# Attention with a state space mixer: state space products placed between the value products

## The chip, the cores and the metric

One Trainium2 chip, one core. The metric is the device time of one execution in microseconds (us). Before the change the median of three executions is 3305.14 us (3303.23 to 3305.94). The engines are called as in the profile: PE is TensorE (matmuls; PEld its weight loads), DVE is VectorE, ACT is ScalarE, POOL is GpSimd, SP is SyncE, which here only issues DMAs.

## The reference, cut to what matters

One layer of a diffusion backbone serves 2048 latent and 256 context tokens of width 1024. A combined projection gives grouped-query attention (8 query heads, 2 key heads of 64) and the input of a complex-diagonal state space (32 channel groups of 16, each with a 64-dimensional complex state, forward and backward). The change touches the stretch in which both are computed at the same time:

```python
s = einsum("bqkgd,bskd->bkgqs", q_blk, k) * scale
p = softmax(s)                                   # over latent and context keys
attn = einsum("bkgqs,bskd->bqkgd", p, v)

xr = einsum("blgh,gph->blgp", u, bbr)            # state inputs (real, imaginary)
_, _, hr, hi = associative_scan(_combine, (ar, ai, xr, xi), reverse=reverse)
y  = einsum("blgp,ghp->blgh", hr, c_re) - einsum("blgp,ghp->blgh", hi, c_im)
...
out = g * sigmoid(g @ w_glu + b_glu)             # g = gelu(y + d * u)
```

After it come the GLU, the output projection, and a SwiGLU feed-forward layer of width 2816.

## The kernel before, in words

**Attention.** There are 20 units: 4 for the context queries (2 key tiles each) and 16 for the latent queries (512 queries, two heads, 20 key tiles of 128 each). `attend` cuts each unit's key tiles into groups of 4, so a latent unit has 5 groups. For each key tile, a *slot* (`slot`) runs the score products of two heads (L266 and L267) into one of two PSUM buffers `st`, and ACT turns them into `p` by an exponential (L269). Then the slot takes steps of a second generator B, which prepares a later unit: above all products of queries and keys whose maximum is wanted (L197, PE) and the reduction of each by DVE (`mx`, L198). These go through a ring `m` of three PSUM banks (`pmx`, bufs=3), which the state space products and a few others share. The slots of group g+1 stand ahead of the *values* of group g (`values`, L283: products of `p` with the values, 16 matmul records a group; L293 and L296 sum up `p` on DVE and POOL). After them come the steps of `finish` (row sums L317, a small chain of DMAs through DRAM for reciprocals, the scaling of the result L335).

**State space.** A third generator, `Sg` (`side`, whose first part is `ssm_gen`), is stepped once in every latent slot, with `X["pos"] = "p"`, and once at a group's end, with `X["pos"] = "v"`: 25 steps a latent unit. It works through 16 units of two channel groups. One unit needs:

- *state inputs* (L1012): for each direction d, 8 matmul records into a bank `m`, copied by ACT into `s` (L1016, L1017); then two DMAs `sw<-s` (L1021, L1022) that swap the halves;
- on DVE a rotation (L1032 to L1034, which writes `s` in place), the scan (L1040), two DMAs `rw<-r` (L1042, L1043), a rotation back (L1047, which writes `r` in place, L1048, L1052), and copies into `h` on ACT (L1059);
- *state outputs* (L982, L984): for each group g, 16 records into a bank `m`, copied by ACT into `ys` (L985), then 16 DMAs `y_scr<-ys` (L990) in all;
- `load` of the next unit: `mst`, `ut`, `et` (2 DMAs), `mot` and `wt` (8 DMAs), each tile with two buffers.

Before the change these are placed by counting steps. A unit takes 20 steps, which is 4 groups: its two input chunks and the two output chunks of the unit before it fall into the four slots of one group, directly behind score products and L197 products; L1032 to L1034, the scan, L1047 with L1048, and L1052 stand at the ends ("v") of four successive groups.

**Order.** The orders of PE and DVE are the program's (`manual_schedule`). ACT, POOL and SP also run strictly in an order fixed when the kernel is built, but there a planner sets it: it goes by its own cost of each instruction and issues, of those that it holds ready, the one that stands earliest in the program. So a load may be issued well ahead of its place, as soon as its buffer is free.

The functions that the change touches are these:

Of the kernel before, what the change touches and what calls it, by code (L numbers as in the profile page):

```python
# [8 lines left out]
F32 = mybir.dt.float32  # L9
F32R = mybir.dt.float32r  # L10
AF = mybir.ActivationFunctionType
# [8 lines left out]
CL, CC = NLAT // T, NCTX // T  # L20
NCH = CL + CC
NE = CL + 1 + CC + 1
# [3 lines left out]
NU = 16  # L26
# [22 lines left out]
def build(nc, tc, I, O):  # L49
    V, S, G, PE = nc.vector, nc.scalar, nc.gpsimd, nc.tensor  # L50
# [61 lines left out]
            f()  # L112

    pb, pe_, pst_, pps = ExitStack(), ExitStack(), ExitStack(), ExitStack()
    X = {"pos": "p"}
    KK = {}

    def attention_open():
        kc = pe_.enter_context(tc.tile_pool(name="kc", bufs=1, side="right"))
        pmx = pps.enter_context(tc.tile_pool(name="pmx", bufs=3, space=PSUM, side="right"))  # L120
        X.update(kc=kc, pmx=pmx)
        X["zb"] = [kc.tile([128, 4, 128], F32, name=f"zb{i}") for i in range(2)]
        for z in X["zb"]:
            G.memset(z, 0.0)

    def run(g):
        for _ in g:
            pass

    def kbuild(kv, t0, t1, part=None):  # L130
        n_ = t1 - t0
        if (kv, t0) not in KK:
            pool = X["kp"] if kv and n_ > 2 else X["kc"]
            khl = pool.tile([128, n_ * 128], F32R, name=f"khl{kv}_{t0}")
# [139 lines left out]
    def values(ui, j):  # L274
        kv, tok, nq, k0, k1, pr_ = units[ui]
        nk = k1 - k0
        if j == 0:
            PV[ui] = X["ppv"].tile([128, 512], F32, name="pv")
            ACC[ui] = {}
        pv, acc = PV[ui], ACC[ui]  # L280
        p = pts.pop((ui, j))
        for h in range(2):
            PE.matmul(pv[64 * h:64 * h + 64, 0:nq], X["vall"][:, k0 + j, 64 * kv:64 * kv + 64], p[:, h, 0:nq],  # L283
                      start=j == 0, stop=j == nk - 1)
        if nk <= 4:
            e = "v"
        elif ui + 1 == len(units):
            e = "v" if j % 3 == 2 or j > 16 else "g"
        else:
            e = "v" if j in VJ else "g"  # L290
        if e in acc:
            if e == "v":
                V.tensor_add(acc[e][:, :, 0:nq], acc[e][:, :, 0:nq], p[:, :, 0:nq])  # L293
            else:
                for h in range(2):
                    G.tensor_add(acc[e][:, h, 0:nq], acc[e][:, h, 0:nq], p[:, h, 0:nq])  # L296
        else:
            acc[e] = p
        if j == nk - 1:
            pvs = X["wk"].tile([128, 512], F32, name="pvs", bufs=2)  # L300
            S.copy(pvs[:, 0:nq], pv[:, 0:nq])
            PEND.append((ui, pvs, acc))
# [43 lines left out]
    def attend(B, Sg):  # L346
        groups = []
        for ui, u_ in enumerate(units):
            js = [(ui, j) for j in range(u_[4] - u_[3])]
            groups += [js[i:i + GROUP] for i in range(0, len(js), GROUP)]  # L350
        st = dict(ready=0, q=0.0, per=0.0, goal=1, s=0.0)
        fin = []

        def step():
            st["ready"] = next(B) or st["ready"]

        def slot(ui, j):
            while st["ready"] < ui:
                step()
            lat = units[ui][2] > 256  # L360
            if lat and not j:
                st["goal"] = min(ui + (2 if ui + 1 < 2 * len(cu) else 1), len(units) - 1)
                st["per"] = sum(prep_steps(i) for i in range(st["ready"] + 1, st["goal"] + 1)) / 19.5
                st["q"] = 0.0
            scores(ui, j)
            st["q"] += st["per"] if lat else 0.0
            while st["q"] >= 1.0:
                st["q"] -= 1.0
                if st["ready"] < st["goal"]:
                    step()  # L370
            if lat:
                X["pos"] = "p"
                next(Sg, None)

        for s_ in groups[0]:
            slot(*s_)
        for gi, g in enumerate(groups):
            if gi + 1 < len(groups):
                for s_ in groups[gi + 1]:
                    slot(*s_)  # L380
            for s_ in g:
                values(*s_)
            for f in list(fin):
                if next(f, "end") == "end":
                    fin.remove(f)
            if gi + 1 < len(groups) and len(groups[gi + 1]) > 2:
                X["pos"] = "v"
                next(Sg, None)
            if PEND:
                fin.append(finish())  # L390
        run(Sg)
        return fin
# [544 lines left out]
    sm = ps_.enter_context(tc.tile_pool(name="sm", bufs=1, side="right"))  # L937
# [5 lines left out]
    def ssm_gen():  # L943
# [7 lines left out]
        h0 = sm.tile([128, 2, 32], F32, name="h0")  # L951
        nc.scalar.dma_start(out=h0, in_=I["h0"])
        stt = sm.tile([128, 2, 32], F32, name="stt")
        dg4 = "p (d g) a -> p d g a"
        fl = "p a b -> p (a b)"
        got = {}
# [32 lines left out]
                for l in range(8):  # L989
                    nc.sync.dma_start(out=y_scr[32 * u + 16 * g:32 * u + 16 * g + 16, l::8, :], in_=ys[16 * l:16 * l + 16, g])  # L990

        def wait(n):
            for _ in range(n):
                yield

        load(0)
        yield from wait(10)
        while X["pos"] != "v":
            yield
        yield  # L1000
        for u in range(NU):
            gu = slice(2 * u, 2 * u + 2)
            mst, mot, wt, et, ut = got[u]
            s = sm.tile([128, 4, NE], F32, name="s", bufs=1)
            s4 = s.rearrange(dg4, d=2)
            S.copy(s4[:, :, :, 0], h0[:, :, gu])
            S.activation(s4[:, :, :, CL + 1], h0[:, :, gu], AF.Copy, scale=0.0)
            for d in range(2):
                sp_ = X["pmx"].tile([128, 2, NCH], F32, name="m")
                for g in range(2):  # L1010
                    for J in range(2):
                        PE.matmul(sp_[:, g, :], mst[:, 2 * d + g, 128 * J:128 * J + 128], ut[:, g, J, :], start=J == 0, stop=J == 1)  # L1012
                a, b = sp_[:, :, 0:CL], sp_[:, :, CL:NCH]
                if d:
                    a, b = a[:, :, ::-1], b[:, :, ::-1]
                S.copy(s[:, 2 * d:2 * d + 2, 1:CL + 1], a)  # L1016
                S.copy(s[:, 2 * d:2 * d + 2, CL + 2:NE], b)  # L1017
                if not d:
                    yield
            sw = sm.tile([128, 4, NE], F32, name="sw", bufs=1)  # L1020
            nc.sync.dma_start(out=sw[0:64], in_=s[64:128])  # L1021
            nc.sync.dma_start(out=sw[64:128], in_=s[0:64])  # L1022
            am = sm.tile([128, 4, NE], F32, name="am", bufs=1)
            G.tensor_mul(am.rearrange(dg4, d=2), lm[:, :, gu, None].to_broadcast([128, 2, 2, NE]), amask[:, None, None, :].to_broadcast([128, 2, 2, NE]))
            yield
            if u:
                yield from outputs(u - 1)
                yield
            else:
                yield from wait(2)  # L1030
            sw4 = sw.rearrange(dg4, d=2)
            V.tensor_mul(s4, s4, et[:, :, 0])  # L1032
            V.scalar_tensor_tensor(sw4, sw4, sg[:, 0:1], et[:, :, 1], op0=ALU.mult, op1=ALU.mult)
            V.tensor_add(s, s, sw)  # L1034
            yield
            if u + 1 < NU:
                load(u + 1)
            yield from wait(4)
            r = sm.tile([128, 4, NE], F32, name="r", bufs=1)
            V.tensor_tensor_scan(r.rearrange(fl), am.rearrange(fl), s.rearrange(fl), 0.0, op0=ALU.mult, op1=ALU.add)  # L1040
            rw = sm.tile([128, 4, NE], F32, name="rw", bufs=1)
            nc.sync.dma_start(out=rw[0:64], in_=r[64:128])  # L1042
            nc.sync.dma_start(out=rw[64:128], in_=r[0:64])  # L1043
            yield
            yield from wait(4)
            r4, rw4 = r.rearrange(dg4, d=2), rw.rearrange(dg4, d=2)
            V.tensor_mul(r4, r4, et[:, :, 0])  # L1047
            V.scalar_tensor_tensor(rw4, rw4, sg[:, 0:1], et[:, :, 1], op0=ALU.mult, op1=ALU.mult)  # L1048
            yield
            yield from wait(4)  # L1050
            h = sm.tile([128, 4, NCH], F32, name="h", bufs=1)
            V.tensor_sub(r.rearrange(fl), r.rearrange(fl), rw.rearrange(fl))  # L1052
            for d in range(2):
                dg = slice(2 * d, 2 * d + 2)
                for lo, hi, e0 in ((0, CL, 0), (CL, NCH, CL + 1)):
                    o = h[:, dg, lo:hi]
                    if d:
                        o = o[:, :, ::-1]
                    S.copy(o, r[:, dg, e0:e0 + hi - lo])  # L1059
            S.copy(stt[:, :, gu], r4[:, :, :, NE - 1])  # L1060
            yield
        yield from outputs(NU - 1)
        yield
        nc.sync.dma_start(out=O["st"], in_=stt.rearrange("p a b -> p (a b)"))
# [83 lines left out]
    Sg = side()  # L1148
# [475 lines left out]
    for i, (c, j) in enumerate(seq):  # L1624
        a, v = aq, vs
# [108 lines left out]
```

## Time and profile before

| what | value |
|---|---|
| median of three executions | 3305.14 us |
| the profiled execution | 3301.18 us |
| its span, first to last instruction | 3299.4 us |
| PE busy | 3063.7 us, 93% of the span |
| DVE, POOL, ACT busy | 77%, 57%, 41% |
| attention with the state space | about 456 to 1466 us of the span |

The span is 1.8 us shorter than the execution. A busy row says only that an engine had something in it; what ends an engine's idle time is read from the waits, and where the work stands from the rows in order of time (the timeline). In a timeline a row may merge several like instructions; its time is that from the first one's start to the last one's end, and matmuls overlap, so the pace is read from the starts of successive rows.

### The profile page before, as it was taken

What the parts mean: (1) busy time and instruction counts of PE and PEld (TensorE: products, weight loads), DVE (VectorE), ACT (ScalarE), POOL (GpSimd) and SP (SyncE); (2) the same over time, 40 slices, a digit from 0 to 9 for tenths busy, and PEclk for the clock granted to TensorE, in tenths of its full rate; (3) what the DMA queues carried; (4) which work ended last, traced back from release to release, by engine and by line L of the source; (5) the groups of instructions that cost most, each with busy time, mean ns of one, the idle gap of its engine ahead of it and who ended that gap; (6) DMA issues with size and microseconds to landing.
All of it is one profiled execution on the core that took longest, in us unless ns stands there. A gap on an engine that the chain in (4) does not pass through costs nothing. (4 is left out here: it accounts for less than half of the span.)

```text
span 3299.4 us, 46241 instructions
## 1 busy us (share of the span) xinstructions
PE 3063.7 (93%) x16087; PEld 2471.0 (75%) x16087; DVE 2552.3 (77%) x3444; ACT 1340.5 (41%) x2378; POOL 1885.7 (57%) x1373
## 2 busy tenths in 40 slices
PE   7898889999999999997997999999999999999797
PEld 5787765555655565557777999899989997878586
DVE  4899766777777887668778877987787877577887
ACT  4333334444444444544555333433343434232332
POOL 3767526655775686774435544554455555354675
PEclk9899999999999999998998999999999999999899
DMA  7565452323333322215565444444434446657653
GB/s 265 181 204 189 144 132 55 88 74 87 85 81 90 82 74 53 65 48 164 186 184 186 130 118 118 134 133 118 120 106 128 122 127 191 155 157 192 174 198 137
DMA packets 515379, 435.19 MB, mean 132 GB/s; under 512 B 106374, under 2 KB 449454, under 8 KB 515148
## 3 DMA queue, kind: packets, MB, share of 16 engines
q1 hardware_dynamic: 498060, 400.57, 40.4%
q0 software_dynamic: 5184, 18.88, 3.4%
q10 hardware_dynamic: 11904, 12.82, 1.2%
q8 instruction: 127, 2.08, 0.3%
q14 instruction: 104, 0.85, 0.1%
HBM read 279.37 MB, written 143.73 MB: 128 GB/s over the span
## 5 line engine op out<-in xcount | busy, mean ns | idle before, releaser
L296 POOL TENSOR_TENSOR p<-p 128x512 f32<-128x512 f32 x442 | 646.2, 1501 | 288.7 <-PE pv L283 185.1
L89 POOL TENSOR_TENSOR op<-wr,op 128x512 fp32r<-128x512 f32 (+1 forms) x297 | 413.9, 1401 | 402.8 <-ACT op L88 375.3
L94 PE MATMUL o<-h,op 128*128 128x384 f32 x1848 | 621.3, 336 | 17.8 <-ACT h L88 17.1
L95 PE MATMUL o<-h,op 128*128 128x384 f32 x1848 | 621.4, 336 | 16.7 <-DVE h L89 16.7
L96 PE MATMUL o<-h,op 128*128 128x384 f32 x1848 | 620.1, 336 | 0.0
L198 DVE TENSOR_REDUCE mx<-m 128x1 f32<-128x512 f32 (+1 forms) x656 | 404.8, 675 | 132.1 <-PE m L197 130.9
L269 ACT ACTIVATE p<-st 128x1024 f32<-128x1024 f32 (+1 forms) x328 | 331.5, 1016 | 242.8 <-PE st L267 233.6
L88 ACT CAST op<-sw 128x512 fp32r<-128x512 f32 (+1 forms) x381 | 232.4, 612 | 327.2 <-PE o L95 260.4
L95 PEld LDWEIGHTS o<-h,op 128*128 128x128 f32 x1848 | 349.4, 189 | 19.4 <-DVE h L89 19.4
L94 PEld LDWEIGHTS o<-h,op 128*128 128x128 f32 x1848 | 349.2, 189 | 19.5 <-ACT h L88 18.6
L96 PEld LDWEIGHTS o<-h,op 128*128 128x128 f32 x1848 | 349.4, 189 | 0.0
L89 POOL TENSOR_TENSOR op<-sw,op 128x512 fp32r<-128x512 f32 (+1 forms) x177 | 261.2, 1480 | 118.1 <-ACT op L88 117.8
L88 ACT CAST op<-wr 128x512 fp32r<-128x512 f32 (+1 forms) x333 | 198.8, 607 | 245.5 <-PE o L95 164.9
L95 PE MATMUL o<-fvm,op 128*128 128x512 f32 x693 | 277.6, 401 | 20.8 <-POOL fvm L89 10.8
L283 PE MATMUL pv<-p,vall 128*64 128x512 f32 (+1 forms) x1312 | 296.4, 593 | 0.0
L94 PE MATMUL o<-fvm,op 128*128 128x512 f32 x693 | 276.4, 400 | 11.2 <-ACT fvm L88 10.5
L266 PE MATMUL st<-qh,khl 128*128 128x512 f32 (+1 forms) x656 | 276.1, 422 | 10.0 <-ACT p L269 8.9
L96 PE MATMUL o<-fvm,op 128*128 128x512 f32 x693 | 273.9, 396 | 0.0
L197 PE MATMUL m<-khl,qh 128*128 128x512 f32 (+1 forms) x656 | 229.7, 421 | 31.6 <-DVE mx L198 20.9
L267 PE MATMUL st<-ql,kho 128*128 128x512 f32 (+1 forms) x656 | 258.3, 395 | 0.0
L283 PEld LDWEIGHTS pv<-p,vall 128*64 128x64 f32 x1312 | 86.8, 136 | 158.2 <-issue 155.0
L89 DVE TENSOR_TENSOR op<-sw,op 128x512 fp32r<-128x512 f32 (+1 forms) x204 | 202.6, 993 | 1.0 <-ACT op L88 1.0
(314 smaller groups left out, 6243.1 us busy)
## 6 DMA issues: line engine op xcount, KB each, us to landing
wr<-w_ffn_in SPq DMA_DIRECT2D x132, 512.0 KB
wm<-w_mod SPq DMA_DIRECT2D x48, 512.0 KB
act_scr<-s SPq DMA_DIRECT2D x99, 192.0 KB
wr<-act_scr SPq DMA_DIRECT2D x36, 512.0 KB
x_scr<-gy POOLq DMA_DIRECT2D x36, 512.0 KB, 6.6
xt<-x SPq DMA_DIRECT2D x34, 512.0 KB
act_scr<-gy SPq DMA_DIRECT2D x90, 192.0 KB
sw<-act_scr SPq DMA_DIRECT2D x54, 256.0 KB
```

What stands on the lines that cost most here:

```text
L88: a = (copy or S.copy)(hi, src)
L89: b = (sub or V).tensor_sub(lo, src, hi.bitcast(F32))
L94: PE.matmul(out, ah, bh, start=first, stop=False)
L95: PE.matmul(out, ah, bl, start=False, stop=False)
L96: return PE.matmul(out, al, bh, start=False, stop=last)
L197: PE.matmul(sp_[:, 0:b - a], qh[:, i * 128:(i + 1) * 128], khl[:, a:b], start=True, stop=True)
L198: V.tensor_reduce(mxs[h][:, i, c:c + 1], sp_[:, 0:b - a], axis=AX.X, op=ALU.max)
L266: PE.matmul(st[:, h, 0:nq], khl[:, kc], qh[:, 0:nq], start=True, stop=False)
L267: PE.matmul(st[:, h, 0:nq], kho[:, kc], ql[:, 0:nq], start=False, stop=True)
L269: S.activation(p[:, :, 0:nq], st[:, :, 0:nq], AF.Exp, scale=0.125)
L283: PE.matmul(pv[64 * h:64 * h + 64, 0:nq], X["vall"][:, k0 + j, 64 * kv:64 * kv + 64], p[:, h, 0:nq], start=j == 0, stop=j == nk - 1)
L296: G.tensor_add(acc[e][:, h, 0:nq], acc[e][:, h, 0:nq], p[:, h, 0:nq])
```

## The change

A third kind of position, "m", is added: behind the second and the fourth value product of a group of four, and `Sg` is stepped there, but only if it asks for it (`X["want"]`). Counting of steps is replaced by `until(pos)`, which yields until the next position of that kind. The input chunks go to the two "m" positions of the same group, and one unit earlier in the program than before: unit u+1's inputs stand between L1047/L1048 and L1052 of unit u. The output chunks go to the second "m" of one group and the first "m" of the next. `load(u + 1)` follows the second output chunk instead of the step after L1034. A unit still takes four groups:

| group end or "m" | before (slot or "v") | after |
|---|---|---|
| group 1 | 2 input and 2 output chunks in the slots; L1032 to L1034 at v | first output chunk at the second m; L1032 to L1034 at v |
| group 2 | load in the first slot; scan, `rw` DMAs at v | second output chunk, `y_scr` DMAs, load at the first m; scan, `rw` DMAs at v |
| group 3 | L1047, L1048 at v | L1047, L1048 at v |
| group 4 | L1052, `h` at v | next unit's two input chunks at both m, `sw` DMAs; L1052, `h` at v |

```diff
-            for s_ in g:
+            for i, s_ in enumerate(g):
                 values(*s_)
+                if len(g) > 2 and i % 2 and X["want"] == "m":
+                    X["pos"] = "m"
+                    next(Sg, None)
...
-        def wait(n):
-            for _ in range(n):
+        def until(pos):
+            X["want"] = pos
+            yield
+            while X["pos"] != pos:
                 yield
+            X["want"] = None
...
+        def inputs(u):
...
             for d in range(2):
+                yield from until("m")
+                if not d:
+                    S.copy(s4[:, :, :, 0], h0[:, :, gu])
+                    S.activation(s4[:, :, :, CL + 1], h0[:, :, gu], AF.Copy, scale=0.0)
                 sp_ = X["pmx"].tile([128, 2, NCH], F32, name="m")
...
-                if not d:
-                    yield
-            sw = sm.tile([128, 4, NE], F32, name="sw", bufs=1)
+            sw = SW[u] = sm.tile([128, 4, NE], F32, name="sw", bufs=1)
             nc.sync.dma_start(out=sw[0:64], in_=s[64:128])
             nc.sync.dma_start(out=sw[64:128], in_=s[0:64])
+
+        load(0)
+        for _ in range(10):
+            yield
+        yield from until("v")
+        yield from inputs(0)
+        yield from until("v")
+        for u in range(NU):
...
-            yield
+            out = outputs(u - 1) if u else iter(())
             if u:
-                yield from outputs(u - 1)
-                yield
-            else:
-                yield from wait(2)
+                yield from until("m")
+                yield from until("m")
+                next(out)
+            yield from until("v")
             V.tensor_mul(s4, s4, et[:, :, 0])
...
-            yield
+            if u:
+                yield from until("m")
+                run(out)
             if u + 1 < NU:
                 load(u + 1)
-            yield from wait(4)
+            yield from until("v")
             V.tensor_tensor_scan(r.rearrange(fl), am.rearrange(fl), s.rearrange(fl), 0.0, op0=ALU.mult, op1=ALU.add)
...
-            yield
-            yield from wait(4)
+            yield from until("v")
             V.tensor_mul(r4, r4, et[:, :, 0])
             V.scalar_tensor_tensor(rw4, rw4, sg[:, 0:1], et[:, :, 1], op0=ALU.mult, op1=ALU.mult)
-            yield
-            yield from wait(4)
+            if u + 1 < NU:
+                yield from inputs(u + 1)
+            yield from until("v")
...
-            yield
+        yield from until("m")
+        yield from until("m")
         yield from outputs(NU - 1)
```

## Rows read from the trace of the kernel before

**Rows 1.** The windows: attention; us, busy PE, PEld, DVE, ACT, POOL; PE clock, DMA.

```profile
456.00:1466.00 1010.00, 951.13 (x4411) 570.61 (x4412) 743.81 (x948) 460.69 (x719) 670.21 (x459) 0.99 0.29 77
```

**Rows 2.** What PE waited for there: total us, times, longest.

```profile
PE m L197 <- DVE mx L198: 17.3, 29, 3.2
...
PE m L1012 <- DVE mx L198: 6.5, 13, 2.3
PE m L982 <- DVE mx L198: 4.5, 14, 0.3
...
PE m L982 <- DVE ql L222: 1.3, 1, 1.3
...
PE m L1012 <- DVE khl L170: 1.2, 1, 1.2
```

**Rows 3.** The windows (as in Rows 1) of three groups, the first with state space products.

```profile
1027.85:1045.98 18.13, 17.10 (x97) 12.11 (x95) 11.66 (x16) 7.83 (x17) 16.34 (x13) 1.00 0.22 56
1068.79:1079.24 10.45, 10.45 (x46) 5.90 (x44) 9.26 (x14) 4.70 (x5) 2.37 (x2) 1.00 0.22 60
...
1014.81:1027.85 13.04, 11.45 (x49) 5.99 (x47) 13.00 (x15) 4.20 (x5) 13.04 (x10) 1.00 0.17 47
```

**Rows 4.** PE in order of time, in the group from 1027.85 (start, us, line).

```profile
1032.52 0.85 PE L197 MATMUL m<-khl,qh 128*128 128x512 f32 x3
1033.70 1.25 PE L1012 MATMUL m<-ut,mst 128*128 128x144 f32 x8 [0.33 <-DVE mx L198]
1034.69 0.49 PE L266 MATMUL st<-qh,khl 128*128 128x512 f32 x1
1035.02 0.40 PE L267 MATMUL st<-ql,kho 128*128 128x512 f32 x1
...
1042.39 3.65 PE L283 MATMUL pv<-p,vall 128*64 128x512 f32 x16
1045.98 0.50 PE L266 MATMUL st<-qh,khl 128*128 128x512 f32 x1
1046.31 0.40 PE L267 MATMUL st<-ql,kho 128*128 128x512 f32 x1
...
1047.01 0.85 PE L197 MATMUL m<-khl,qh 128*128 128x512 f32 x3
1047.69 0.39 PE L266 MATMUL st<-qh,khl 128*128 128x512 f32 x1
```

**Rows 5.** PE in the group from 1177.39: a chunk that met no wait.

```profile
1181.21 1.15 PE L1012 MATMUL m<-ut,mst 128*128 128x144 f32 x8
1182.10 0.49 PE L266 MATMUL st<-qh,khl 128*128 128x512 f32 x1
```

**Rows 6.** SP's queue in the groups from 1027.85: DMA issues, start, us, count.

```profile
1038.76 10.90 SPq L990 DMA_DIRECT2D y_scr<-ys  x16
...
1051.04 0.53 SPq L966 DMA_DIRECT2D ut<-u_scr  x1
...
1053.38 4.65 SPq L971 DMA_DIRECT2D wt<-kd_scr  x8
```

**Rows 7.** DVE in order of time, from the scan to L1047, one unit.

```profile
1106.88 2.33 DVE L1040 TENSOR_TENSOR_SCAN r<-am,s 128x584 f32<-128x584 f32 x1
...
1115.37 1.83 DVE L1047 TENSOR_TENSOR r<-r,et 128x584 f32<-128x584 f32 x1
```

**Rows 8.** PE in the same group: where its values begin.

```profile
1103.79 3.65 PE L283 MATMUL pv<-p,vall 128*64 128x512 f32 x16
```

**Rows 9.** The second swap DMA of a unit on SP.

```profile
731.01 0.59 SPq L1022 DMA_DIRECT2D sw<-s  x1
```

**Rows 10.** DVE: the instruction that waited for that DMA.

```profile
735.60 1.84 DVE L1032 TENSOR_TENSOR s<-s,et 128x584 f32<-128x584 f32 x1 [2.40 <-DMA sw<-s]
```

**Rows 11.** ACT behind one unit's scan (L1006 needs the scan's end).

```profile
1004.56 0.20 ACT L1006 COPY s<-h 128x4 f32<-128x4 f32 x1 [3.93 <-DMA wt<-kd_scr]
1004.66 0.58 ACT L301 COPY pvs<-pv 128x512 f32<-128x512 f32 x1
```

More of the change, by code (lines that the diff above doesn't have):

```diff
@@ L114, in build @@
     pb, pe_, pst_, pps = ExitStack(), ExitStack(), ExitStack(), ExitStack()
-    X = {"pos": "p"}
+    X = {"pos": "p", "want": None}
     KK = {}
@@ L990, in outputs @@
                     nc.sync.dma_start(out=y_scr[32 * u + 16 * g:32 * u + 16 * g + 16, l::8, :], in_=ys[16 * l:16 * l + 16, g])
-        def wait(n):
-            for _ in range(n):
+        def until(pos):
+            X["want"] = pos
+            yield
+            while X["pos"] != pos:
                 yield
-        load(0)
-        yield from wait(10)
-        while X["pos"] != "v":
-            yield
-        yield
-        for u in range(NU):
+            X["want"] = None
+        S_, SW = {}, {}
+        def inputs(u):
             gu = slice(2 * u, 2 * u + 2)
-            mst, mot, wt, et, ut = got[u]
-            s = sm.tile([128, 4, NE], F32, name="s", bufs=1)
+            mst, _, _, _, ut = got[u]
+            s = S_[u] = sm.tile([128, 4, NE], F32, name="s", bufs=1)
             s4 = s.rearrange(dg4, d=2)
-            S.copy(s4[:, :, :, 0], h0[:, :, gu])
-            S.activation(s4[:, :, :, CL + 1], h0[:, :, gu], AF.Copy, scale=0.0)
             for d in range(2):
+                yield from until("m")
+                if not d:
+                    S.copy(s4[:, :, :, 0], h0[:, :, gu])
+                    S.activation(s4[:, :, :, CL + 1], h0[:, :, gu], AF.Copy, scale=0.0)
                 sp_ = X["pmx"].tile([128, 2, NCH], F32, name="m")
@@ L1017, in ssm_gen @@
                 S.copy(s[:, 2 * d:2 * d + 2, CL + 2:NE], b)
-                if not d:
-                    yield
-            sw = sm.tile([128, 4, NE], F32, name="sw", bufs=1)
+            sw = SW[u] = sm.tile([128, 4, NE], F32, name="sw", bufs=1)
             nc.sync.dma_start(out=sw[0:64], in_=s[64:128])
             nc.sync.dma_start(out=sw[64:128], in_=s[0:64])
+        load(0)
[5 more added lines that the diff above has]
+        for u in range(NU):
+            gu = slice(2 * u, 2 * u + 2)
+            et = got[u][3]
+            s, sw = S_.pop(u), SW.pop(u)
             am = sm.tile([128, 4, NE], F32, name="am", bufs=1)
             G.tensor_mul(am.rearrange(dg4, d=2), lm[:, :, gu, None].to_broadcast([128, 2, 2, NE]), amask[:, None, None, :].to_broadcast([128, 2, 2, NE]))
-            yield
+            out = outputs(u - 1) if u else iter(())
             if u:
-                yield from outputs(u - 1)
-                yield
-            else:
-                yield from wait(2)
-            sw4 = sw.rearrange(dg4, d=2)
+                yield from until("m")
+                yield from until("m")
+                next(out)
+            yield from until("v")
+            s4, sw4 = s.rearrange(dg4, d=2), sw.rearrange(dg4, d=2)
             V.tensor_mul(s4, s4, et[:, :, 0])
@@ L1048, in ssm_gen @@
             V.scalar_tensor_tensor(rw4, rw4, sg[:, 0:1], et[:, :, 1], op0=ALU.mult, op1=ALU.mult)
-            yield
-            yield from wait(4)
+            if u + 1 < NU:
+                yield from inputs(u + 1)
+            yield from until("v")
             h = sm.tile([128, 4, NCH], F32, name="h", bufs=1)
@@ L1060, in ssm_gen @@
             S.copy(stt[:, :, gu], r4[:, :, :, NE - 1])
-            yield
+        yield from until("m")
+        yield from until("m")
         yield from outputs(NU - 1)
```

## The prediction, made before the change was run

> **What bounds the kernel now.** I read the windows first. The stage that the change touches lasts 1010 us, and PE is busy for 951.1 of them [rows 1]: PE sets its length, and 58.9 us of idle PE are all that a new order of the same instructions can give back, about 1.8% of the whole. DVE stands at 743.8 and is the next engine, POOL (670.2) and ACT (460.7) have room. Next the waits of PE in that stage. The longest by total is L197 on the reduction `mx` (17.3 us, 29 times): the ring of three banks is full until DVE has reduced the oldest. State space products use the same ring, and they wait for the same thing: L1012 6.5 us in 13 times, L982 4.5 us in 14, and single waits of 1.3 and 1.2 us on L222 and L170 [rows 2]. Third, groups one by one: a plain one takes 10.45 us with no PE idle; the one with four state space chunks takes 18.13 [rows 3]. The chunks' own time is 5.3 us (48 records at 0.89/8 [rows 5]), so 2.4 of the 7.7 us between them are something else. Fourth, that group in order of time. A wait stands behind three L197 in a row: those three have just taken all three banks, and the chunk wants a fourth [rows 4].
>
> **The change, part by part.** PE's instructions stay as they are; only places change.
>
> *The waits in front of the chunks.* Removed on record: 6.5 + 4.5 + 1.3 + 1.2 = 13.5 us [rows 2]. Behind the second value product PE has run half of a values phase since the last L197, 3.59/2 = 1.8 us [rows 4], and in that time DVE, which gets no new reduction, has only to free one bank of three (bounds for what is left to wait: 0, and the present 13.5 if DVE were late by more than that). I take 0: in the plain group DVE keeps up, busy for 9.26 of 10.45 us [rows 3].
>
> *What the record leaves out.* The idle time counts from the modelled end of the matmul before. Without a wait three L197 take 0.68 us until the next matmul starts (1047.01 to 1047.69); here it took 1.18 (1032.52 to 1033.70), 0.50 lost against 0.33 on record, and the eight records behind it took 0.99 instead of 0.89 [rows 4, 5]. So a common wait of 0.33 costs 0.60. Over the 27 common ones that is up to 27 x 0.27 = 7.3 us more; some are longer and need no such correction, so I take 6 (bounds 0 and 7.3).
>
> *Switches of PE.* The first score product behind a chunk takes 0.33 us (1034.69 to 1035.02) where 0.23 is the pace (0.68/3), and so does the first behind the values (1045.98 to 1046.31): 0.10 for a switch [rows 4]. No row shows values, chunk, values; I take 0.10 for either border (bounds 0 and 0.33, a whole first record). Before: 64 chunks with one extra switch each, 6.4 us. After: 32 chunks in the middle of the values with two (6.4) and 32 at their end with one, since the switch to the scores was there anyway (3.2). Net +3 (bounds -3 and +18).
>
> *DVE's relief.* A chunk between slots gave DVE time to catch up with reductions. The former group of chunks becomes a plain one: 0 lost as in the second group of rows 3, or as much as in the third, 13.04 against 10.45, of which about 1 is the row sums' products. I take 2 us in all: the values phases now last 1.8 us longer in three of four groups, just where DVE does L1032 to L1034, the scan and L1052 (bounds 0 and 15 x 1.4 = 21).
>
> *Loads and DMAs.* `ut` can only be reused after the second output chunk. It was issued 1051.04, behind 10.9 us of `y_scr` issues [rows 6]; it will have two groups, some 25 us, until the next input chunk reads it, so nothing waits (if that cover went: one stall of PE a unit, as long as the lateness). The `sw` DMAs now have a whole group, 10 us and more, in place of the rest of the slots; the one wait for them, 2.40 us on DVE [rows 10], goes, worth nothing on PE. ACT's copy of `h0` (L1006) has waited 3.93 us for the scan while queued ahead of its place [rows 11]; the scan is not earlier now, so this stays: 0. The state space ends about two groups later and with it the GLU's preparation moves towards the end of the stage; it still has groups left there: 0 (bounds -5 and +5, half a plain group).
>
> *Sum.* -13.5 - 6 + 3 + 2 = -14.5 us. The profiled execution takes 3301.2 us (span 3299.4 and 1.8 around it), so it would take 3286.7. The median of the runs is 4.0 above the profiled one; the forecast for the median is 3305.1 - 14.5 = 3290.6 us.
>
> **Rivals.** *First, slower: SP's queue comes between scan and L1047.* Both `rw` DMAs must have read `r` before L1047 may overwrite it, and DVE's order is fixed, so the next slots' reductions stand behind L1047, and with three banks PE stands behind them. Before, the `y_scr` DMAs and the loads were issued a whole group ahead of the scan. Now the second half of the `y_scr` DMAs, `ut`, `mot` and `wt` become ready 1.8 us before the values end, close to the scan's end, and are earlier in the program than `rw`: if the planner sees the scan end after the chunk, `rw` goes behind all of them. Its price, from the unit shown: the values begin at 1103.79, L1047 at 1115.37, so 11.6 us behind [rows 7, 8], and 13.4 with a chunk (1.8) in between. The queue: half the values (1.8), the chunk (1.8), half of 10.90 (5.45), `ut` and `mot` (0.6 each), `wt` (4.65) [rows 6], the first half of `rw` (0.55): the second is issued at 15.5 us; a like DMA was waited for until 4.6 us behind its issue (731.01 to 735.60) [rows 9, 10], so it has read `r` at 20.1. DVE stalls 6.7 us in this unit, and 4.1 where the group is 2.6 longer, as the third of rows 3. PE has banks for about one slot, (10.45 - 3.59)/4 = 1.7 us, and loses 2.4 to 5.0, say 3.5. In all 15 units that have such a queue: +53 - 14.5 = +38, 3343 us; in eleven, +24, 3329. Four units eat up the gain, from six on it is slower by over 0.2%. For it: the places in the program. Against: ACT has L1006, which needs the scan, queued ahead of L301, which is ready when the values end [rows 11]; so to the planner the scan ends within the values, and perhaps before the chunk does. No row decides this.
>
> The Trainium skill (DMA: Bandwidth & Descriptors, "Anatomy of one DMA") puts the fixed part of a DMA at about 2.0 us, most of it the receipt of the write. By it the second `rw` DMA would be done some 2.3 us sooner than by the row (its 146 KB add an estimated 0.3), and the rival in all 15 units would come to about +4 us, no change. The trace does not agree here: 4.6 us [rows 9, 10]; I keep the row.
>
> *Second, no change: the waits only move.* DVE owes the same reductions, and in the slots it now has fewer PE microseconds beside them, so the 19.5 us appear again in front of L197, which already has the largest total [rows 2]. With the switches that is +3: 3308, at best 3303. For it: 13.04 us of the third group, in which DVE is busy for 13.00; against it: the second group, whose 10.45 us PE fills [rows 3].
>
> **How the numbers follow.** A difference under 0.2% (6.6 us) can't be told from no change here. Forecast 0.48: 3281 to 3299, nearly all of it faster. First rival 0.30: 3312 to 3343 where it holds in six units or more (0.27), within 0.2% in fewer. Second rival 0.17: mostly no change. The end of the stage, either way: 0.05. Together faster 0.50, same 0.19, slower 0.31. The range, 3281 to 3330, leaves out half of the first rival's upper part and a little at the bottom; the forecast's own is 3281 to 3299.
>
> **What would show it.** Right: no waits of L1012 and L982 for `mx`, chunks of 0.89 and 1.8 us inside the values, former chunk groups at some 10.5 to 11.5 us and the values phases longer instead, L197's total about as before, the stage near 995 us. The first rival: `rw` issued behind `wt` on SP, L1047 waiting for a DMA, long waits of L197 in the group behind it. The second: L197's total near 30 us and the stage's PE idle time unchanged. The forecast is wrong if PE's idle time in the stage does not fall by at least 8 us.

## The result, and the profile after

The changed kernel takes 3343.5 us (median of four, 3338.5 to 3350.7) beside 3305.5 us of the kernel before on the same chip: a ratio of 1.0119 with a 95% interval of 1.0102 to 1.0136, so 38 us slower. 3291 us was forecast, and the result lies outside the range of 3281 to 3330; 3343 us was what the first rival gave for fifteen units. The profiled execution took 3343.5 us, its span is 3341.7.

**Where the time is.** Stage starts are the starts of groups. The 82 groups that begin at 456 us take 994.94 us before and 1035.95 after; what lies behind them differs by 1.4 (1848.1 and 1849.5). Twenty groups in the middle that hold the same work, five state space units, take 250.50 and 266.10. First the kernel before in the same windows (columns as in [rows 1]), then after; the last three windows of after are one group, its part up to a stall, and the 5.5 us behind it.

```profile
456.34:1451.28 994.94, 936.61 (x4339) 562.29 (x4339) 735.87 (x944) 454.54 (x711) 655.49 (x450) 0.99 0.29 77
975.88:1226.38 250.50, 239.32 (x1128) 145.76 (x1126) 197.95 (x246) 109.20 (x177) 170.83 (x117) 1.00 0.31 82
```

```profile
456.20:1492.15 1035.95, 964.81 (x4363) 573.77 (x4361) 735.93 (x948) 460.39 (x714) 656.46 (x450) 0.97 0.29 74
990.65:1256.75 266.10, 249.40 (x1128) 150.41 (x1126) 196.81 (x246) 110.51 (x177) 170.83 (x115) 0.96 0.30 77
1046.30:1063.97 17.67, 14.90 (x65) 9.25 (x63) 12.42 (x15) 6.48 (x12) 17.67 (x13) 0.90 0.23 56
1046.30:1052.47 6.17, 3.50 (x17) 2.38 (x15) 3.31 (x4) 3.22 (x4) 6.17 (x5) 1.00 0.28 63
1052.47:1058.00 5.53, 5.43 (x15) 3.88 (x15) 3.92 (x7) 1.56 (x2) 5.53 (x6) 0.69 0.40 108
```

In the twenty groups PE is idle for 16.7 us instead of 11.2 and busy for 10.1 us longer, at a granted clock of 0.96 instead of 1.00, with the same 1128 records. So only about one third of the loss is idle time; the rest is busy time, most of it by the lower clock.

**What PE and DVE wait for.** The waits of PE after (us in total, times, longest), from 456 to 1506 us:

```profile
PE m L197 <- DVE mx L198: 40.0, 33, 7.1
PE m L197 <- DVE ql L222: 9.6, 8, 4.7
```

The waits of the chunks for `mx` [rows 2] are gone, as forecast; L197's own went from 17.3 to 40.0 us. Two more waits behind DVE grew: that of L197 for `ql`, from 1.6 to 9.6 us, and one of L165 for `khl`, of 4.5 us, where before there was none. DVE's waits in the same stretch say what DVE was doing:

```profile
DVE pvs L335 <- DMA rT<-rr_scr: 35.2, 7, 9.5
DVE r L1062 <- DMA rw<-r: 16.3, 5, 4.5
DVE rr L329 <- DMA rr<-rs_scr: 13.2, 4, 6.8
```

L1062 is L1047 of before: it never waited for a DMA there, and waits 16.3 us now. That is the rival's wait. The other two are not: L335 and L329 belong to `finish`, the chain of small DMAs for the row sums. Before, they were shorter (456 to 1466 us):

```profile
DVE pvs L335 <- DMA rT<-rr_scr: 19.7, 8, 5.8
...
DVE rr L329 <- DMA rr<-rs_scr: 6.9, 1, 6.9
```

SP's queue after shows both, first around a `finish`, then around L1062 of a later unit:

```profile
916.82 0.47 SPq L331 DMA_DIRECT2D rr_scr<-rr  x1
917.84 0.37 SPq L969 DMA_DIRECT2D ut<-u_scr  x1
919.73 5.02 SPq L993 DMA_DIRECT2D y_scr<-ys  x8
...
925.42 4.36 SPq L974 DMA_DIRECT2D wt<-kd_scr  x8
929.82 0.48 SPq L331 DMA_DIRECT2D rr_scr<-rr  x1
...
931.63 0.59 SPq L1059 DMA_DIRECT2D rw<-r  x1
932.33 0.54 SPq L333 DMA_DIRECT2D rT<-rr_scr  x1
...
1040.81 5.21 SPq L974 DMA_DIRECT2D wt<-kd_scr  x8
...
1046.67 0.59 SPq L1059 DMA_DIRECT2D rw<-r  x1
```

DVE in order of time at the two places, idle time in brackets:

```profile
924.17 1.88 DVE L293 TENSOR_TENSOR p<-p 128x1024 f32<-128x1024 f32 x1
935.53 0.69 DVE L335 TENSOR_TENSOR pvs<-pvs,rT 128x512 f32<-128x512 f32 x1 [9.48 <-DMA rT<-rr_scr]
936.14 0.76 DVE L1062 TENSOR_TENSOR r<-r,et 128x584 f32<-128x584 f32 x1
...
1042.94 1.77 DVE L293 TENSOR_TENSOR p<-p 128x1024 f32<-128x1024 f32 x1
1049.16 0.91 DVE L1062 TENSOR_TENSOR r<-r,et 128x584 f32<-128x584 f32 x1 [4.45 <-DMA rw<-r]
```

In one `finish` the two stores of the reciprocals, `rr_scr`, are 13 us apart (916.82 and 929.82): `ut`, eight `y_scr`, `mot` and eight `wt` are issued between them. L335 waits, and L1062 and the reductions of the next slots stand behind it on DVE. In 11 of the 15 units with a next load both `rw` DMAs are issued behind `wt`; in five units DVE then waits for `rw` itself.

**What a stall costs PE.** PE in the group of the second place (a score product is a record of L266 or L267):

```profile
1048.70 0.39 PE L266 MATMUL st<-qh,khl 128*128 128x512 f32 x1
1048.93 0.40 PE L267 MATMUL st<-ql,kho 128*128 128x512 f32 x1
1049.30 0.50 PE L197 MATMUL m<-khl,qh 128*128 128x512 f32 x1
1052.47 1.09 PE L197 MATMUL m<-khl,qh 128*128 128x512 f32 x2 [2.68 <-DVE mx L198]
...
1054.01 0.63 PE L266 MATMUL st<-qh,khl 128*128 128x512 f32 x1
1054.43 0.63 PE L267 MATMUL st<-ql,kho 128*128 128x512 f32 x1
```

Before the stall a score product starts every 0.23 us, behind it every 0.42. The window behind the stall has a granted clock of 0.69 where the part ahead of it has 1.00: part of it at the lower level of 1.2 GHz. The group takes 17.67 us; the same group without a stall takes 12.75 (first experiment). Of the 4.92 us between them, 2.68 are idle and about 1.7 the clock (5.43 us busy x 0.31). Not every stall has this price. One of 2.67 us that ended at 785.30 was followed by a clock of 1.00:

```profile
785.28:791.00 5.72, 5.59 (x23) 3.22 (x23) 5.65 (x10) 2.05 (x2) 5.72 (x6) 1.00 0.40 105
```

What tells the two apart, these rows do not show.

### The profile page after: what moved, and what is told of

Read it like the earlier page. It is cut to its first block, busy times and chain, and to the rows that moved or that the text cites. A ratio compares the mean times of both kernels' runs of the same rounds, so it can differ in the third digit from the quotient of the medians.

```text
span 3341.7 us, 46240 instructions
## 1 busy us (share of the span) xinstructions
PE 3089.2 (92%) x16087; PEld 2481.0 (74%) x16087; DVE 2546.6 (76%) x3444; ACT 1346.0 (40%) x2380; POOL 1889.5 (57%) x1373
## 5 line engine op out<-in xcount | busy, mean ns | idle before, releaser
L296 POOL TENSOR_TENSOR p<-p 128x512 f32<-128x512 f32 x442 | 650.8, 1508 | 323.1 <-PE pv L283 165.5
L283 PE MATMUL pv<-p,vall 128*64 128x512 f32 (+1 forms) x1312 | 305.7, 600 | 0.0
L197 PE MATMUL m<-khl,qh 128*128 128x512 f32 (+1 forms) x656 | 238.5, 433 | 59.5 <-DVE mx L198 43.6
L266 PE MATMUL st<-qh,khl 128*128 128x512 f32 (+1 forms) x656 | 277.7, 424 | 4.4 <-ACT p L269 3.1
L267 PE MATMUL st<-ql,kho 128*128 128x512 f32 (+1 forms) x656 | 263.6, 403 | 0.0
L197 PEld LDWEIGHTS m<-khl,qh 128*128 128x128 f32 x656 | 126.9, 195 | 139.1 <-DVE mx L198 98.1
```

The lines of the kernel that those rows point to most:

```text
L197: PE.matmul(sp_[:, 0:b - a], qh[:, i * 128:(i + 1) * 128], khl[:, a:b], start=True, stop=True)
L266: PE.matmul(st[:, h, 0:nq], khl[:, kc], qh[:, 0:nq], start=True, stop=False)
L267: PE.matmul(st[:, h, 0:nq], kho[:, kc], ql[:, 0:nq], start=False, stop=True)
```

## The experiments

**The theories.** Q: the cost is SP's queue behind the second output chunk (`ut`, `mot`, eight `y_scr`, eight `wt`, about 10 us) ahead of what DVE waits for; the new places on PE are themselves a small gain. P: the new places on PE cost the time. The first four kernels take one part each. All are edits of the changed kernel; the kernel before was run on the same chip each time. The code is cut to what matters, and its comments stand in this text alone.

**`rw` ahead of stores and loads (e1_rw_first).** PE's order is that of the changed kernel.

```diff
                 if not g:                  # in outputs()
                     yield
+            yield                          # the stores are a step of their own
...
             if u:
                 yield from until("m")
-                run(out)
-            if u + 1 < NU:
-                load(u + 1)
+                next(out)                  # the second output chunk alone
             yield from until("v")
...
             nc.sync.dma_start(out=rw[64:128], in_=r[0:64])
+            run(out)                       # the y_scr stores
+            if u + 1 < NU:
+                load(u + 1)
```

> The changed kernel, but the y_scr DMAs and the next unit's loads stand behind the rw DMAs in the program, so SP issues rw right behind the scan (at most ut goes first). Theory Q (SP's queue keeps rw, and so L1047 and the reductions behind it, waiting): the waits of L197 on mx fall from 40.0 to some 17 us, no L1062 waits for rw, the attention stage is about 40 us shorter than in the changed kernel and the time within 0.3% of before (ratio 0.996 to 1.003). Theory P (the products among the values cost it themselves, by switches of PE and the relief that DVE lost): nothing of this changes, ratio 1.010 to 1.013.

Measured: 3303.7 us, ratio 0.9986 (0.9973 to 0.9998). All of the loss is gone, with the same order on PE. Windows of this kernel (the stage, the twenty groups, the group that stalled above):

```profile
456.05:1445.98 989.93, 945.67 (x4357) 558.98 (x4356) 749.10 (x947) 459.60 (x714) 666.73 (x450) 0.99 0.30 78
...
972.36:1220.62 248.26, 243.22 (x1128) 146.14 (x1126) 203.50 (x248) 110.19 (x177) 174.58 (x115) 0.99 0.32 82
...
1025.76:1038.51 12.75, 12.75 (x64) 8.04 (x63) 11.81 (x15) 6.45 (x11) 12.75 (x9) 1.00 0.25 60
```

Its waits of PE and DVE, 456 to 1500 us; none of L1064 (the former L1062) for `rw` is left:

```profile
PE m L197 <- DVE mx L198: 18.0, 30, 2.2
...
DVE pvs L335 <- DMA rT<-rr_scr: 10.0, 5, 4.0
...
DVE rr L329 <- DMA rr<-rs_scr: 6.9, 1, 6.9
```

P falls: between this kernel and the changed one lie 46.0 us of the stage (1035.95 to 989.93), with the same order on PE and DVE. Of these, 26.9 are idle time of PE (71.1 against 44.3 us); the other 19.1 are busy time, at a granted clock of 0.97 against 0.99. The planner's order on ACT differs in a few places too, which was not separated.

**`rw` on another queue (e2_rw_act).** The stores and loads stay where the change put them.

```diff
-            nc.sync.dma_start(out=rw[0:64], in_=r[64:128])
-            nc.sync.dma_start(out=rw[64:128], in_=r[0:64])
+            nc.scalar.dma_start(out=rw[0:64], in_=r[64:128])
+            nc.scalar.dma_start(out=rw[64:128], in_=r[0:64])
```

> The changed kernel with the two rw DMAs issued from ACT's queue instead of SP's; everything else as in the changed kernel. Theory Q: as the first experiment, ratio 0.997 to 1.004, with some 1 us of ACT a unit for two issues. Theory P: 1.010 to 1.013.

Measured: 3322.4 us, ratio 1.0047 (1.0028 to 1.0065), above what Q expected. Its stage (the 82 groups) and its waits of DVE:

```profile
456.09:1473.17 1017.08, 955.30 (x4335) 566.05 (x4333) 736.23 (x944) 459.92 (x713) 659.43 (x450) 0.98 0.29 75
```

```profile
DVE pvs L335 <- DMA rT<-rr_scr: 37.6, 7, 10.8
DVE rr L329 <- DMA rr<-rs_scr: 13.0, 3, 6.8
```

DVE no longer waits for `rw`, and 18.9 of the 46.0 us come back; by the ratios of the runs it is about 24 of 44. The waits of `finish` stay, and five groups behind the first still take 18.4 to 20.9 us. So Q holds, but `rw` is only part of what the queue delays; the waits in sight for the other 27.1 us (1017.08 against 989.93) are those of `finish`. What the two issues cost on ACT's queue is in the 27.1 too.

**The inputs alone, and the outputs alone (e3_inputs_only, e4_outputs_only).** In the first kernel only the input chunks stand between values, and outputs, stores and load go by counted steps; in the second it is the other way round.

```diff
 # inputs only
-                yield from until("m")
-                yield from until("m")
+                for _ in range(3):
+                    yield
                 next(out)
+                yield
+                run(out)                   # a chunk in each of two slots
...
-            if u:
-                yield from until("m")
-                run(out)
             if u + 1 < NU:
+                yield
                 load(u + 1)
 # outputs only
-                yield from until("m")      # in inputs()
+                yield
...
         for u in range(NU):
+            yield from inputs(u)
```

> Only the input chunks stand among the values; output chunks, y_scr DMAs and loads are back in the slots, a group ahead of the scan. Theory Q: rw is free again, no waits for it, ratio 0.996 to 1.002. Theory P: half of the chunks still stand among the values, about half of the loss, ratio 1.005 to 1.007.

> Only the output chunks (with y_scr DMAs and loads behind them) stand among the values as in the changed kernel; input chunks are back in two slots. Theory Q: the queue ahead of rw is the same as in the changed kernel, ratio 1.009 to 1.014. Theory P: half of the loss, 1.005 to 1.007.

Measured: inputs only 3305.5 us, 0.9995 (0.9982 to 1.0008); outputs only 3339.2 us, 1.0096 (1.0077 to 1.0115), with DVE waits of 41.6 us for `rT` and 14.8 for `rw`. The loss comes with the outputs, whose stores and load go with them.

**Half of the queue each time (e6_ystores_first, e7_loads_first).** From the first experiment: the stores go back ahead of `rw` (first kernel), or the loads do (second).

```diff
 # stores first: behind the second output chunk, ahead of the scan
-                next(out)
+                run(out)
 # loads first: at the same place
                 next(out)
+            if u + 1 < NU:
+                load(u + 1)
```

> Half of the queue taken away: the second half of the y_scr stores may stand ahead of rw as in the changed kernel, mot and wt behind it. In the planned order of SP the second rw DMA stands behind the eight y_scr stores in two of five alignments, in the others rw is first or the finish chain is. Theory Q (the loss is the length of SP's queue ahead of rw and of the finish chain's rr and rT): 5 us of queue instead of 10 in part of the units, 3306 to 3322 us. Rival P (the loss comes from where PE's chunks stand, whose order is the same as in the changed kernel): 3338 to 3345.

> The other half: ut, mot and the eight wt loads stand ahead of rw in three of five alignments, the second half of the y_scr stores behind it. Theory Q: 5.2 us of queue instead of 10.2: 3308 to 3325 us, DVE waiting for rw at most 2 us at a time instead of 4.5. Rival P (place of the chunks on PE): 3338 to 3345.

Measured: 3306.6 us, 0.9993 (0.9982 to 1.0004), and 3303.8 us, 0.9980 (0.9970 to 0.9990). Both lie at the lower end of Q's range or below it. In the second, both `rw` DMAs stand behind `wt` in the same 11 units as in the changed kernel, and DVE waits for `rw` in neither. Half a queue, some 5 us, costs nothing that can be measured; the whole one costs 38 us. So the price is not by length. The likely reason, which was argued and not isolated: DVE has some microseconds of its own work ahead of these waits, and only what is over counts. The time goes with DVE's three waits together (`rT`, `rr`, `rw`): they sum to between 16.9 and 26.6 us in the kernel before and in the four of 3304 to 3307 us, to 50.6 in that of 3322, and to 64.7 and 70.5 in those of 3343 and 3339.

**`rw` and the finish chain off SP (e8_rw_rt_off).** The second experiment, and the seven DMAs of `finish` on POOL's queue.

```diff
-            nc.sync.dma_start(out=rs_scr[ui, :, 0:nq], in_=rT[0:128:64, 0:nq])
+            nc.gpsimd.dma_start(out=rs_scr[ui, :, 0:nq], in_=rT[0:128:64, 0:nq])
 # rr, rr_scr and rT likewise
```

> The changed kernel with both rw DMAs on the ACT queue as in e2_rw_act and the finish chain's DMAs (row sums out and back, reciprocals out and back) on the POOL queue; y_scr and the loads stay where the change put them. Theory Q with two victims: the finish chain is what e2 still lost (3322 against 3304 of e1), so 3300 to 3310 us, with the DVE waits for rT down from 37 to under 12 us. Rival: what is left in e2 is the changed place of the y_scr stores and loads themselves (DMA engines shared), 3320 to 3325. Risk: POOL waits in order for each landing and its additions come late, seen as PE waiting for p or DVE for POOL.

Measured: 3386.6 us, 1.0235 (1.0217 to 1.0254), far above both expected ranges; the risk named last is what came. Its waits of PE (456 to 1500 us):

```profile
PE m L197 <- ACT s L1022: 23.8, 4, 6.4
...
PE st L266 <- ACT p L269: 11.4, 6, 4.9
```

DVE waits 33.9 us in 9 times for `rr` (6.9 in one before), and ACT stands behind DVE (8.75 us before its copies of `h` at 808.83). On POOL its sums come between: four of L296 take 4.93 us between the loads of `rr` (802.15) and the stores of `rr_scr` (808.11). The kernel shows that a later finish chain costs PE dearly; whether the chain alone explains the rest of the second experiment it does not show.

**Each chunk at the end of a group's values (e5_ends_only).** From the first experiment: no chunk in the middle of the values, one at the end of each of four groups, the two input chunks on either side of L1062; the load goes ahead of the stores, both still behind `rw`.

```diff
-                if len(g) > 2 and i % 2 and X["want"] == "m":
+                if len(g) > 2 and i == len(g) - 1 and X["want"] == "m":
```

> rw first as in e1_rw_first, then the loads, then the second half of the y_scr stores; each of the four chunks now stands alone at the end of the values of one group, none in the middle of the values. Theory S (switches inside the values cost about 0.33 us on the first score behind them and 0.2 to 0.4 us on chunk and values): 32 chunks lose the switch in the middle, 32 x 0.2 to 0.4 = 6 to 13 us less than e1_rw_first, so 3291 to 3298 us, 0.995 to 0.998 of before. Rival (switches cost nothing measurable; only the stalls counted, and these are gone in e1 already): same as e1, 3303 +- 3. Second rival: the input chunks now flank r4's multiplication, and a later h or sw makes DVE wait: over 3306, seen as DVE waits on DMA sw or ACT.

Measured: 3314.2 us, 1.0015 (1.0002 to 1.0028). The time is that of the second rival, but not by its waits: DVE waits for no `sw`. The regular groups became shorter, the twenty 243.78 us against 248.26, but two single waits ate it up. Waits of PE:

```profile
PE m L218 <- DMA qs<-q_scr: 10.9, 1, 10.9
PE m L165 <- DMA kt<-k_scr: 9.9, 1, 9.9
```

Both loads stood on SP behind `wt` and `y_scr` (`kt` was issued 938.45, behind 9.1 us of these): a third victim of the same queue. So the next kernel (e9_ends_late_stores) issues the second half of the stores one group later, and the one after it (e10_rest_late) `mot` and `wt` too.

```diff
 # first
             if u + 1 < NU:
                 load(u + 1)
-            run(out)                       # the stores
...
             V.scalar_tensor_tensor(rw4, rw4, sg[:, 0:1], et[:, :, 1], op0=ALU.mult, op1=ALU.mult)
+            run(out)
 # second, on top of it: mot and wt are taken out of load
+            if u + 1 < NU:
+                load_rest(u + 1)           # mot and wt
             run(out)
```

> e5_ends_only with the second half of the y_scr stores issued one group later, behind r4's multiplications, so that kt's loads and half of the first qs loads stand ahead of them on SP. Reason: e5's regular groups run 0.9 us per unit shorter than e1's (16 groups 195.25 against 198.94 us), but it has two single stalls of PE for loads that stood on SP behind wt and y_scr, kt 9.9 us and qs 10.9 us. If these two are the whole of its excess: 3314 less 10 to 20, 3294 to 3304 us. Rival (e5 is slow for another reason, chunks at each end of values delay the chain): 3310 or more, with the kt and qs waits gone.

> e9_ends_late_stores with mot and the eight wt loads, which the next unit's output chunks need only a unit later, issued behind r4's multiplications too, ahead of the y_scr stores; ut stays behind rw. In the planned order of SP kt's loads now stand ahead of wt. If what e9 still loses is queue time in front of kt (5.7 us) and qs (5.6 us): 3302 less 5 to 11, 3291 to 3297 us. Rival (these loads were not what held kt and qs, or mot and wt come too late for the output chunks): 3302 or more, PE waiting for wt or still for kt.

Measured: 3301.9 us, 0.9982 (0.9970 to 0.9994), with 5.7 and 5.6 us of these two waits left; then 3296.4 us (3288.0 to 3298.6), 0.9948 (0.9934 to 0.9963). The second beats both kernels; its time is in the expected range. Its windows:

```profile
456.09:1435.92 979.83, 939.88 (x4362) 562.90 (x4360) 751.41 (x946) 458.05 (x714) 672.52 (x450) 0.99 0.30 78
...
969.45:1211.11 241.66, 238.26 (x1129) 145.18 (x1128) 204.15 (x246) 109.90 (x179) 175.28 (x115) 1.00 0.33 85
```

`kt` is issued at 915.31, ahead of `wt`, and PE's longest wait for it is 2.4 us; `qs` is no longer among PE's longer waits. SP in this kernel:

```profile
914.07 0.54 SPq L969 DMA_DIRECT2D ut<-u_scr  x1
...
915.31 2.21 SPq L154 DMA_DIRECT2D kt<-k_scr  x4
```

Its profiled stage is 15.1 us shorter than before, its span only 4.8: what lies behind the stage took 1858.7 us there, and 1848 to 1861 in the profiles of the others, with the same code. That is a spread between profiled executions; its cause is open. On the chip of this run the median of the kernel before is 3310.7 us, and the profile of before that is used here is of an execution of 3301.2.

## Why the prediction was wrong

**Loads and DMAs: the step that failed.** It says that `ut` has 25 us until its reader, "so nothing waits". That is true of `ut`, and the step stops there: it follows each moved DMA to its own reader, and not each DMA that is queued behind the moved ones. So the queue stood in the sum with 0; putting `rw` ahead of it and changing nothing on PE or DVE gave back 46.0 us of the stage. The prediction knew of this for `rw` alone and gave it 0.30 because "no row decides" the planner's order. The argument against it, that L1006 stands ahead of L301 on ACT [rows 11], bore on when the planner sees the scan end; in 11 of 15 units the order came out the other way.

**The price of the queue.** The rival's 3.5 us a unit came near: 46.0 us in 11 units with the queue ahead of `rw` are 4.2 each. But the mechanism was half of it. DVE waited for `rw` in five units, not in eleven or fifteen. `rw` alone accounts for 18.9 us (second experiment); in the other 27.1 the only new DMA waits of DVE are those of the finish chain, which the prediction does not name. That this chain is the whole of the 27.1 was not isolated. And the rival counted idle time only, while the lower clock was over a third of the price of the stall looked at, and 19.1 of the 46.0 us are busy time. The rival with eleven units gave 3329. That 3343, its figure for fifteen, came out is luck: two errors of one sign are in it, the price (46.0 instead of 11 x 3.5 = 38.5) and the gain (5 instead of 14.5).

**The DMA's own time.** The prediction kept 4.6 us [rows 9, 10] for the second `rw` DMA against the estimate from the Trainium skill (DMA: Bandwidth & Descriptors, "Anatomy of one DMA"), 2.3 us. That section gives its figure for DMAs that GpSimd issues, and `rw` is issued by SP. The trace after has 2.49 us (issued 1046.67, L1062 at 1049.16), and 2.5 to 3.5 in the other four waits of L1062. So the Trainium skill's figure comes near the trace here, and the row kept was too high; why L1032 waited until 4.6 us is open. The conclusion drawn from that figure, no change in all, still fell: the queue, not the transfer, is long.

**The waits in front of the chunks.** Right: no wait of the chunks for `mx` is left. In the first experiment, where the queue is out of the way, PE's idle time in twenty groups falls from 11.2 to 5.0 us, about 20 us over 16 units, and L197's total in the whole stage is 18.0 (17.3 before). The second rival, that these waits only move, is refuted by that.

**Switches of PE: mis-sized.** Forecast: 0.2 us a unit more than before. In the first experiment PE is busy 243.22 instead of 239.32 us in five units, 0.78 a unit, but part of its window is at the lower clock (0.99 in all). In the two kernels with half of the queue, PE's order is the same and the clock is 1.00 throughout:

```profile
979.04:1226.66 247.62, 241.93 (x1129) 144.90 (x1127) 199.97 (x246) 110.13 (x177) 174.09 (x115) 1.00 0.33 83
...
977.68:1223.97 246.29, 241.85 (x1128) 144.95 (x1127) 201.30 (x246) 110.33 (x177) 172.48 (x115) 1.00 0.32 83
```

There it is 0.5 a unit. A chunk in the middle and one at the end, in the first experiment:

```profile
1032.61 1.94 PE L283 MATMUL pv<-p,vall 128*64 128x512 f32 x8
1034.48 1.25 PE L1018 MATMUL m<-ut,mst 128*128 128x144 f32 x8
1035.66 1.94 PE L283 MATMUL pv<-p,vall 128*64 128x512 f32 x8
1037.52 1.25 PE L1018 MATMUL m<-ut,mst 128*128 128x144 f32 x8
1038.51 0.49 PE L266 MATMUL st<-qh,khl 128*128 128x512 f32 x1
```

From start to start the chunk in the middle takes 1.18 us, the one at the end 0.99, and one behind L197 took 0.89 [rows 5]; the two halves of the values take 1.87 and 1.86 where they took 3.59 together [rows 4]. A chunk in the middle costs 1.18 - 0.89 + 0.14 = 0.43 us of switches, where the forecast had 0.20; one at the end costs 0.10, as forecast. The last kernel, which has none in the middle, is busy 238.26 us, 3.6 less than the two kernels above, in ten such chunks: 0.36 each. So the waits won nearly 20 us, as the forecast's first two terms said (19.5), and the switches took about 0.5 x 16 = 8 of it, not 3. The whole stage gained less than that leaves, and less than the forecast 14.5: it takes 994.94 us before, 989.93 in the first experiment, and 992.9 and 995.2 in the kernels with the loads first and the stores first. These are single executions; what took the difference is open.

**DVE's relief and the end of the stage.** DVE's 2 us can't be told apart in these numbers. (Their upper bound, 15 x 1.4, would be 15 x 1.6 by the row and the 1 us that it names; nothing rests on it.) The state space ending later cost nothing visible: what lies behind the stage took 1849.5 us after and 1848.1 before.

## What to carry to other kernels

When instructions move, write down the in-order queue of each engine that issues DMAs for one whole period, and ask of every DMA now queued behind the moved ones who waits for it, not only of the moved ones; here three chains (a scan's exchange, row sums, the loads of keys and queries) hung on one queue. Issue what a consumer is waiting for first and bulk stores and far prefetches behind it; 5 us of queue were free here and 10 were not. A chunk of matmuls that is put between two phases of others pays for each change of phase (0.43 us in the middle here, 0.10 at the end), so put it at a change that is there already.

## What the runs showed of the hardware

A stall of 2.68 us on PE was followed by a granted clock of 0.69 over 5.5 us, with score products starting every 0.42 us instead of 0.23; the group took 4.9 us longer in all. Another of 2.67 us was followed by a clock of 1.00. SP took 0.54 to 0.65 us for each of these small DMAs (eight `y_scr` in 5.02, eight `wt` in 4.36 to 5.21), so sixteen of them were 10 us in which nothing else of that queue started. A matmul chunk of eight records has taken 0.89, 0.99 or 1.18 us without any wait on record, by what stands ahead of it and behind it.
